# Weight low halves, key rope and convolution blocks rearranged in a two-block transformer kernel

## The chip, the core and the metric

The kernel runs on one core of a Trainium2 chip. The metric is the device time of one execution in microseconds (us); 1730.88 us is the median of three runs before the change, which lay between 1729.36 and 1731.35 us.

## What is computed

The reference is two transformer parts on 256 tokens of width 1024, all in float32:

- a first block: `x + mixed @ w_o`, where `mixed` joins a stick-breaking attention of 8 heads and a latent attention (MLA) of 8 heads, followed by a PEER layer. In MLA each key is `concat(k_nope, k_rot)`: 64 numbers of its own head and 32 numbers, `k_pe`, that all heads share. The key is normalised (`rms_norm` with `k_norm`) and only then the last 32 are turned by `rope`. PEER scores 16 sets of 128 sub-keys with `w_q`, picks 16 experts of 16384 per head by two rounds of `top_k`, and sums `coef * v[idx]`;
- two further layers, each modulated by a vector: layer 0 is a differential attention with a Fourier branch and a SwiGLU, layer 1 a conformer convolution (`a * sigmoid(g)`, a depthwise convolution of 31 taps, layer norm, silu, a projection) and a SwiGLU. A last `rmsnorm` ends it.

## The kernel before, in words

**Split products.** The program works transposed: features on partitions, the 256 tokens along the free axis. Nearly every weight product is made of three rounded products. A weight tile of 128x1024 numbers is loaded, ScalarE copies it to the rounded type (`hi`, `_hi`, L602), and the remainder `src - hi` (`lo`, L615, L644) is the low half. TensorE then adds `hi*x_hi`, `hi*x_lo` and, last, `lo*x_hi` (`steps_t`, L662). So a tile of eight contraction steps is 16 matmuls with `hi`, then 8 with `lo`.

**Who makes the low half.** `plan` (L532) lists every weight tile in the order of use, with a number `cut`: columns below `cut` are made by VectorE, the others by GpSimd (POOL). Before, the cut is 512 (half and half) for the first block's mixer, for six of the 16 `w_pq` tiles and for the differential layer; 0 (all POOL) for the other `w_pq` tiles and the first `EARLY` = 40 of the 128 `peer_u` tiles; 1024 (all VectorE) elsewhere. `next_w` (L628) hands out the next tile and issues loads, `hi` and `lo` ahead: `self.los` says how many tiles ahead the low halves go out.

**Order.** The engines run their queues in order; the order is that in which the Python program issues. In the attention stages `weave` (L237) mixes tasks (one per head) between the steps of a main stream of weight products, by a cost model of TensorE's time.

**First mixer** (`first_mixer`, L835). Query, key and value projections; `kpe` (the shared rope part, L882) is copied by a DMA on the SP queue to all eight heads' keys (L883). `qk_norm` (L1067) is a task per pair of heads, for keys and for queries: square on ScalarE, a product with ones, Ln and Exp on ScalarE, one multiplication on VectorE, then the rope: two VectorE multiplications (32 and 16 rows, 512 columns) and two POOL operations (48 rows). The keys' rope is turned thus four times, once per pair.

**PEER** (`peer`, L1134). 16 `w_pq` tiles; from the fifth on each is followed by the top-16 search of two rows of scores, a chain of short VectorE instructions (`Select.top`, L1925). Then come `EARLY` tiles of `peer_u`, beside which VectorE ends the selection (`selection`, L1181); the rest of `peer_u` runs in pieces of ten matmuls (`mid`, L1214; `steps`, L1238) between the 64 groups that build the coefficient table, three pieces a group, ten pieces before the first (`PRE` = (2, 8)). Last come 128 `peer_v` tiles, beside which the modulation and the context norm (`context`, L1398) are computed.

**Differential layer** (`diff`, L1416). Six query tiles; the rope of a query tile (`rope`, L1435) is four VectorE and two POOL operations, issued two tiles later; then the values (`values`, L1471) and the weave.

**Conformer** (`conformer`, L1728). For each of eight blocks of channels: two weight tiles, a sigmoid gate, and 31 taps that are split over TensorE (diagonal matrices, `conv_pe`, `PE_TAPS`, in plain float32), ScalarE with POOL (`conv_pool`, `POOL_TAPS`) and VectorE (`conv`, the rest). `finish` joins the three; `center`, `square` and `total` make the sums of the layer norm. Then a short serial chain makes its factor, and the projection follows.

Of the kernel before, what the change touches and what calls it, by code (L numbers as in the profile page):

```python
# [16 lines left out]
ALU = mybir.AluOpType  # L17
# [28 lines left out]
PRE = (2,8)  # L46
# [31 lines left out]
def _vec_layout():  # L78
    at = 0
    for name, n in (  # L80
        ("attn_norm", 8), ("cq_norm", 3), ("ckv_norm", 2), ("q_norm", 1), ("k_norm", 1),
# [364 lines left out]
class Net:  # L446
# [85 lines left out]
    def plan(self):  # L532
        a, w = self.a, []
        add = lambda name, cut, *idx: w.append((a[name][idx] if idx else a[name], cut))
        for i in range(6):
            add("w_in", 512, i)
        for i in range(4):
            add("w_sbv", 512, i)
        for kind, i in MAINS:
            if kind == "k":  # L540
                add("w_ukn", 512)
            elif kind == "v":
                add("w_ukv_v", 512)
            elif kind == "m":
                add("w_uq", 512, i)
            else:
                add("w_in", 512, 6 + i)
                add("w_in", 512, 10 + i)
        for name in ("w_om", "w_os"):
            for i in range(4):  # L550
                add(name, 512, i)
        for i in range(16):
            add("w_pq", 512 if i < 6 else 0, i)
# [4 lines left out]
        for i in range(DHEADS):  # L558
            add("ev_qkf", 512, i)
        for i in range(4):  # L560
            add("ev_v", 512, 0, i)
        for i in range(DHEADS):
            add("ev_qkf", 512, DHEADS + i)
        for i in range(4):
            add("ev_v", 512, 1, i)
        for i in range(2):
            add("ev_qkf", 512, 2 * DHEADS + i)
        for i in range(KD):
            add("ev_out", 512, (i + 6) % KD)
# [265 lines left out]
    def first_mixer(self, ctx):  # L835
# [29 lines left out]
        nk = norm(ckv, 2, 15 * U, rk)  # L865
        for i in range(3):
# [16 lines left out]
        nc.sync.dma_start(km[64:QR], self.bc(kpe[64:QR], HEADS))  # L883
# [17 lines left out]
        for _ in rope:  # L901
            pass

# [16 lines left out]
        def main():  # L920
# [72 lines left out]
        for p in range(4):  # L993
            for i, (n, which, x) in enumerate((("k", "k_norm", km), ("q", "q_norm", qm))):
                s = ar(2 * U + (2 * p + i) * 512 if p < 2 else 11 * U + (2 * p + i - 4) * 512, 512)[:QR]
                tasks.append(Task((which, p), self.qk_norm(s, which, x, p, qe if i else ke), [(n, p)], "qk"))
# [70 lines left out]
    def qk_norm(self, sq, which, x, p, ext):  # L1067
# [4 lines left out]
        if "q" in OFFA:  # L1072
            nc.gpsimd.tensor_tensor(sq, xs, xs, op=ALU.mult)
        else:
            nc.scalar.activation(sq, xs, AF.Square)
# [6 lines left out]
        nc.vector.scalar_tensor_tensor(xs, xs, self.vec(which, rows=QR), sq, op0=ALU.mult, op1=ALU.mult)  # L1082
        for o, i in ((slice(64, 96), slice(96, P)), (slice(96, QR), slice(64, 80))):
# [50 lines left out]
    def peer(self, ctx):  # L1134
# [111 lines left out]
        steps(PRE[0])  # L1246
# [853 lines left out]
```

## Time and profile before

| what | value |
|---|---|
| median of three runs | 1730.88 us (1729.36 to 1731.35) |
| the profiled execution's own time | 1729.7 us |
| its span, first to last instruction | 1727.9 us |
| TensorE (PE) busy | 1652.9 us, 96% |
| VectorE (DVE) busy | 1357.9 us, 79% |
| ScalarE (ACT) busy | 1010.0 us, 58% |
| GpSimd (POOL) busy | 418.4 us, 24% |
| mean granted TensorE clock | 0.984 |

The span leaves 1.8 us outside the first and last instruction, and the profiled execution is 1.2 us below the median. Busy shares are means over stages with different limits, so they are read by stage.

### The profile page before, as it was taken

To read this page: it belongs to the slowest core of one execution; us is meant where nothing else is said; L and a number is where in the kernel's file an instruction comes from. 1 tells how busy PE (TensorE), PEld (TensorE's weight loads), DVE (VectorE), ACT (ScalarE), POOL (GpSimd) and SP (SyncE) were. 2 spreads that over 40 slices of the span, in tenths; PEclk is the share of its full clock that TensorE was granted. 3 is DMA by queue.
4 is the path that set the end of the run, shared out by engine and by line. 5 is a ranking of instruction groups with operands and counts; after the bars stand their busy time and mean duration, and the time that the engine had idled before them with its cause. 6 is when DMAs were issued, how large, how long until landed. Compare 5 with 4: busy or idle time off the path is not lost.

```text
span 1727.9 us, 33717 instructions
## 1 busy us (share of the span) xinstructions
PE 1652.9 (96%) x12964; PEld 1580.2 (91%) x12964; DVE 1357.9 (79%) x2395; ACT 1010.0 (58%) x1925; POOL 418.4 (24%) x275
## 2 busy tenths in 40 slices
PE   7989999989999999999999988999999989799998
PEld 6778999989999999999999987788999989699998
DVE  7787899987778875778888778978877799785555
ACT  5756555468777765444555553566555578564444
POOL 3553679910000000000110027533000048410000
PEclk9999999999999999999999999999999999899999
DMA  5332455544445456776878755125788733145553
GB/s 181 117 111 79 135 169 186 175 139 163 159 162 169 160 171 229 248 241 236 299 257 308 271 174 174 52 90 188 273 309 308 261 116 103 50 159 184 185 190 127
DMA packets 88112, 315.66 MB, mean 183 GB/s; under 512 B 10000, under 2 KB 11024, under 8 KB 87696
## 3 DMA queue, kind: packets, MB, share of 16 engines
q1 hardware_dynamic: 87952, 313.51, 53.7%
q8 instruction: 103, 1.69, 0.4%
q14 instruction: 57, 0.47, 0.1%
HBM read 312.03 MB, written 1.05 MB: 181 GB/s over the span
## 4 chain that ended last, share of the span: by engine, by line
PE 63%; DVE 23%; ACT 5%; issue 3%; DMA 3%; POOL 2%; SPq 0%; DVEq 0%; ACTq 0%; POOLq 0%
PE mm L178 34%; PE at L178 28%; DVE a L208 19%; ACT a L208 2%; DMA a<-in_peer_v_dram 2%; ACT wh L208 2%; POOL a L208 1%; DVE praw L208 1%; DMA a<-in_w_dram 1%; DVE xT L208 1%; ACT L208 1%; PE at L183 0%; DVE gb L208 0%; DVE adaw L208 0%; DMA a<-in_w_in_dram 0%
## 5 line engine op out<-in xcount | busy, mean ns | idle before, releaser
L178 PE MATMUL mm<-a,wh 128*128 128x256 f32 (+3 forms) x4752 | 663.7, 289 | 17.0 <-ACT wh L208 11.1
L208 ACT ACTIVATE wh<-a 128x1024 fp32r<-128x1024 f32 (+3 forms) x491 | 514.9, 1053 | 279.1 <-DMA a<-in_w_dram 138.2
L178 PEld LDWEIGHTS mm<-a,wh 128*128 128x128 f32 (+1 forms) x4752 | 608.0, 191 | 33.7 <-ACT wh L208 11.8
L208 DVE TENSOR_TENSOR a<-a,wh 128x1024 fp32r<-128x1024 f32 (+3 forms) x440 | 516.9, 1182 | 118.4 <-ACT wh L208 116.7
L178 PE MATMUL mm<-a,a 128*128 128x256 f32 (+5 forms) x2596 | 415.1, 297 | 24.5 <-DVE a L208 17.7
L178 PEld LDWEIGHTS mm<-a,a 128*128 128x128 f32 (+1 forms) x2596 | 355.2, 191 | 38.5 <-DVE a L208 19.2
L178 PE MATMUL at<-a,wh 128*128 128x256 f32 x2152 | 283.6, 282 | 9.1 <-DVE a L208 5.2
L208 POOL TENSOR_TENSOR a<-a,wh 128x512 fp32r<-128x512 f32 (+3 forms) x118 | 228.0, 1943 | 244.9 <-PE at L178 116.8
L178 PEld LDWEIGHTS at<-a,wh 128*128 128x128 f32 x2152 | 268.4, 190 | 11.7 <-DVE a L208 6.0
L208 POOL TENSOR_TENSOR a<-a 128x256 f32<-128x256 f32 (+3 forms) x44 | 73.6, 1673 | 751.4 <-ACT a L208 749.6
L178 PE MATMUL at<-a,a 128*128 128x256 f32 (+6 forms) x1288 | 211.1, 297 | 5.8 <-POOL a L208 4.3
L178 PEld LDWEIGHTS at<-a,a 128*128 128x128 f32 (+2 forms) x1288 | 171.5, 190 | 22.6 <-issue 9.1
L208 ACT ACTIVATE a<-a 128x256 fp32r<-128x256 f32 (+6 forms) x222 | 100.9, 464 | 110.1 <-DVE a L208 88.1
L208 POOL TENSOR_TENSOR a<-a,a 128x256 f32<-128x256 f32 (+3 forms) x75 | 89.9, 1204 | 304.8 <-ACT a L208 277.5
L208 DVE TENSOR_TENSOR a<-a,a 128x256 fp32r<-128x256 f32 (+5 forms) x191 | 123.7, 648 | 26.0 <-ACT a L208 21.4
L208 ACT ACTIVATE a<-mm 128x256 f32<-128x256 f32 (+30 forms) x170 | 59.0, 351 | 107.3 <-PE mm L178 106.9
L178 PE MATMUL at<-fgh,wh 128*128 128x256 f32 x352 | 86.3, 282 | 2.2 <-ACT wh L208 2.2
L178 PE MATMUL at<-fgl,wh 128*128 128x256 f32 x352 | 86.1, 282 | 0.0
L208 ACT ACTIVATE oh<-oh,rest 128x128 f16<-128x128 f16 x256 | 81.0, 396 | 0.0
L208 DVE TENSOR_TENSOR a<-a,at 128x176 f32<-128x176 f32 (+48 forms) x111 | 36.1, 351 | 54.4 <-PE at L178 34.8
L178 PEld LDWEIGHTS at<-fgh,wh 128*128 128x128 f32 x352 | 66.4, 189 | 2.6 <-ACT wh L208 2.6
L178 PEld LDWEIGHTS at<-fgl,wh 128*128 128x128 f32 x352 | 66.3, 188 | 0.0
(157 smaller groups left out, 1544.9 us busy)
## 6 DMA issues: line engine op xcount, KB each, us to landing
a<-in_w_dram SPq DMA_DIRECT2D x132, 512.0 KB, 4.2
a<-in_peer_u_dram SPq DMA_DIRECT2D x128, 512.0 KB, 3.3
a<-in_peer_v_dram SPq DMA_DIRECT2D x128, 512.0 KB, 4.3
adaw<-in_ada_dram SPq DMA_DIRECT2D x48, 512.0 KB, 4.3
a<-in_ada_dram SPq DMA_DIRECT2D x48, 512.0 KB, 5.1
a<-in_pw_dram SPq DMA_DIRECT2D x24, 512.0 KB, 3.3
a<-in_w_pq_dram SPq DMA_DIRECT2D x16, 512.0 KB, 3.3
a<-in_ev_qkf_dram SPq DMA_DIRECT2D x14, 512.0 KB, 3.4
```

What stands on the lines that cost most here:

```text
L178: return self.engine.matmul(out, w, x, **kw)
L208: return f(*args, **kw)
```

## The change

Seven edits, shortened here where a pattern repeats; `...` marks what is left out.

1. Low halves of all mixer tiles and of all `w_pq` tiles on VectorE; `EARLY` 40 to 44; low halves go out two tiles ahead in the first mixer's projections.
2. The keys' shared part is scaled and turned once, before the attention, and copied to the heads later; `qk_norm` for keys then only scales.
3. The pieces of `mid` ahead of the first group are spread (two after each step).
4. `context` moves one step every four `peer_v` tiles, not every two.
5. The queries' ropes go out beside the values.
6. Ten more convolution taps on TensorE, two fewer on POOL; so VectorE's fall from 97 to 89.
7. The last blocks of the conformer in another order; the layer norm's `r` and `dp` in two PSUM banks; the conformer's `Pre` is set up ahead of the last accumulation.

```diff
-PE_TAPS = (7, 8, 8, 8, 8, 8, 11, 14)
+PE_TAPS = (8, 9, 9, 9, 9, 9, 14, 15)
-POOL_TAPS = (11, 11, 11, 11, 11, 11, 7, 6)
-EARLY = 40
+POOL_TAPS = (11, 11, 11, 11, 11, 9, 7, 6)
+EARLY = 44
-PRE = (2,8)
+PRE = 2
...
         for i in range(6):
-            add("w_in", 512, i)
+            add("w_in", D, i)
...
         for i in range(16):
-            add("w_pq", 512 if i < 6 else 0, i)
+            add("w_pq", D, i)
...
         nk = norm(ckv, 2, 15 * U, rk)
+        self.los = 2
...
-        nc.sync.dma_start(km[64:QR], self.bc(kpe[64:QR], HEADS))
...
         for _ in rope:
             pass
+        self.los = 1
+        kr, kt = ar(0, T), ar(T, T)
+        self.copy(kr[64:QR], kpe[64:QR], scale=self.vec("k_norm")[64:QR])
+        for o, i in ((slice(64, 80), slice(96, QR)), (slice(96, QR), slice(64, 80))):
+            nc.vector.tensor_tensor(kt[o], kr[i], self.sinE[i], op=ALU.mult)
+        nc.vector.tensor_tensor(kr[64:QR], kr[64:QR], self.cosE[64:QR], op=ALU.mult)
+        for o in (slice(64, 80), slice(96, QR)):
+            nc.vector.tensor_tensor(kr[o], kr[o], kt[o], op=ALU.add)
...
                     yield from qk(p)
+                    if p == 0:
+                        nc.sync.dma_start(km[64:QR], self.bc(kr[64:QR], HEADS))
...
-            nc.scalar.activation(sq, xs, AF.Square)
+        n = QR if kpe is None else 64
+        nc.scalar.activation(sq[:n], xs[:n], AF.Square)
+        if kpe is not None:
+            nc.scalar.activation(v3(sq[64:]), self.bc(kpe[64:QR], 2), AF.Square)
...
         nc.vector.scalar_tensor_tensor(xs, xs, self.vec(which, rows=QR), sq, op0=ALU.mult, op1=ALU.mult)
+        if kpe is not None:
+            return
...
-        steps(PRE[0])
+        steps(PRE)
         for g in range(2):
             sel[g].place(slots, g)
+            steps(2)
...
             one_hots(b)
-        steps(PRE[1])
+            steps(2)
...
-            if cg is not None and i % 2 == 1:
+            if cg is not None and i % 4 == 3:
                 next(cg, None)
...
             if i > 1:
-                rope(qT[:, i - 2])
                 next(side, None)
...
         for n, _ in enumerate(values(0, "at")):
-            if n in (1, 3):
-                rope(qT[:, DHEADS - 2 + n // 2])
-            if n % 2 == 0:
+            if n < DHEADS:
+                rope(qT[:, n])
+            else:
                 next(steps, None)
...
+        j = KD - 1
+        self.los = 0
+        pa, ba = pre.scaled(*pre.tile(), sp)
+        conv_pe(j - 1)
+        conv_pool(j - 1)
+        conv(j - 1)
+        square(0, 4)
+        gate(j, pa, ba)
+        total(0, 4)
+        self.copy(ub[j % 2], us[j % 3])
+        finish(j - 2)
+        center(4, 6)
+        conv_pe(j)
+        conv_pool(j)
+        finish(j - 1)
+        conv(j)
+        square(4, 6)
+        total(4, 6)
         self.table(AF.Exp)
...
-        rd = self.bank()
-        r, dp = rd[:, :T], rd[:, T:]
+        r, dp = (self.bank()[:, :T] for _ in range(2))
```

`gate(j, pa, ba)` is the second weight tile of a block with its sigmoid and the gating multiplication, as they stood in the loop. In the loop's last round `center(0, 4)` now goes out ahead of `conv_pool`.

## Rows read from the trace of the kernel before

**Rows 1.** The page's first part: busy time, share of the span, instructions of each engine.
```profile
PE 1652.9 (96%) x12964; PEld 1580.2 (91%) x12964; DVE 1357.9 (79%) x2395; ACT 1010.0 (58%) x1925; POOL 418.4 (24%) x275
```

**Rows 2.** Busy time by stage: stretch, length, PE, PEld, DVE, ACT, POOL (xcount), granted clock.
```profile
52.00:120.00 68.00, 59.97 (x377) 49.79 (x377) 58.32 (x76) 45.21 (x86) 41.44 (x30) 0.92 0.29 91
...
202.70:235.60 32.90, 32.90 (x283) 32.90 (x282) 30.25 (x155) 17.46 (x31) 25.72 (x12) 1.00 0.49 161
235.60:359.40 123.80, 117.59 (x988) 116.61 (x986) 119.33 (x248) 63.08 (x89) 106.67 (x39) 1.00 0.53 175
...
1009.00:1066.00 57.00, 47.43 (x298) 43.92 (x297) 52.09 (x88) 24.78 (x44) 34.14 (x29) 0.94 0.52 176
...
1412.00:1472.00 60.00, 57.58 (x372) 53.24 (x372) 56.23 (x102) 46.26 (x99) 46.28 (x25) 0.97 0.29 95
```

**Rows 3.** The same view for three short stretches with the granted clock at 0.50.
```profile
106.00:112.80 6.80, 6.03 (x25) 5.53 (x25) 6.48 (x16) 4.00 (x7) 2.19 (x3) 0.50 0.22 77
358.60:365.40 6.80, 6.05 (x28) 6.05 (x29) 6.56 (x19) 3.47 (x4) 0.00 (x0) 0.50 0.24 74
1037.80:1044.60 6.80, 5.05 (x23) 5.05 (x24) 5.95 (x12) 2.06 (x5) 4.74 (x5) 0.50 0.32 101
```

**Rows 4.** Timeline at 30 us: start, us, engine, operation [idle before <-releaser].
```profile
29.83 0.68 DVE L208 TENSOR_TENSOR a<-a,wh 128x512 fp32r<-128x512 f32 x1
...
30.57 1.22 PE L178 MATMUL mm<-a,a 128*128 128x256 f32 x4 [0.93 <-DVE a L208]
30.65 1.27 POOL L208 TENSOR_TENSOR a<-a,wh 128x512 fp32r<-128x512 f32 x1 [2.14 <-issue]
...
31.98 1.22 PE L178 MATMUL mm<-a,a 128*128 128x256 f32 x4 [0.18 <-POOL a L208]
```

**Rows 5.** Waits, first mixer, 52 to 120 us: us in total, times, longest.
```profile
PE mm L178 <- DVE a L208: 3.1, 2, 2.4
PE mm L178 <- POOL a L208: 2.7, 3, 1.0
...
PE at L178 <- POOL a L208: 2.2, 1, 2.2
```

**Rows 6.** Groups by form, 52 to 120 us: xcount | busy us, mean ns.
```profile
L208 DVE TENSOR_TENSOR a<-a,a 16x512 f32<-16x512 f32 x8 | 11.4, 1430 | 0.1
L208 DVE TENSOR_TENSOR a<-a,wh 128x512 fp32r<-128x512 f32 x9 | 10.7, 1193 | 3.0 <-ACT wh L208 2.9
L208 DVE TENSOR_TENSOR a<-a,a 32x512 f32<-32x512 f32 x8 | 9.8, 1228 | 0.8
...
L208 POOL TENSOR_TENSOR a<-a,a 48x512 f32<-48x512 f32 x16 | 24.5, 1536 | 3.3 <-DVE a L208 2.2
```

**Rows 7.** Timeline: a whole low half on VectorE with POOL idle.
```profile
1006.06 1.23 DVE L208 TENSOR_TENSOR a<-a,wh 128x1024 fp32r<-128x1024 f32 x1 [1.35 <-ACT wh L208]
```

**Rows 8.** Timeline: TensorE after the early tiles.
```profile
359.35 1.01 PE L178 MATMUL mm<-a,a 128*128 128x256 f32 x3 [4.35 <-DVE a L208]
```

**Rows 9.** Waits, `peer_v` stage, 640 to 1009 us.
```profile
PE at L178 <- ACT wh L208: 3.4, 6, 1.1
```

**Rows 10.** Timeline: the differential layer's fifth query tile.
```profile
1036.94 0.74 PE L178 MATMUL mm<-a,a 128*128 128x258 f32 x4 [2.42 <-DVE a L208]
1039.55 1.23 PE L178 MATMUL mm<-a,a 128*128 128x258 f32 x4 [1.87 <-POOL a L208]
```

**Rows 11.** Waits, query tiles and values, 1009 to 1066 us.
```profile
PE at L178 <- POOL a L208: 2.2, 4, 0.9
```

**Rows 12.** Groups by form, conformer's loop, 1412 to 1472 us.
```profile
L208 DVE SCALAR_TENSOR_TENSOR gb<-at,vecs,gb 128x256 f32<-128x256 f32 x31 | 14.7, 475 | 0.0
```

**Rows 13.** Timeline: TensorE at the conformer's end.
```profile
1472.66 6.31 PE L178 MATMUL mm<-a,a 128*128 128x256 f32 x28 [1.14 <-DVE a L208]
...
1487.11 0.70 PE L178 MATMUL at<-a,cons 128*128 128x256 f32 x2 [3.21 <-POOL a L208]
1488.46 4.05 PE L178 MATMUL at<-a,cons 128*128 128x256 f32 x10 [0.65 <-ACT a L208]
```

More of the change, by code (lines that the diff above doesn't have):

```diff
@@ L993, in first_mixer @@
         for p in range(4):
-            for i, (n, which, x) in enumerate((("k", "k_norm", km), ("q", "q_norm", qm))):
+            for i, (n, which, x) in enumerate((("k", "k_nope", km), ("q", "q_norm", qm))):
                 s = ar(2 * U + (2 * p + i) * 512 if p < 2 else 11 * U + (2 * p + i - 4) * 512, 512)[:QR]
-                tasks.append(Task((which, p), self.qk_norm(s, which, x, p, qe if i else ke), [(n, p)], "qk"))
+                tasks.append(Task((n + "_norm", p), self.qk_norm(s, which, x, p, qe, None if i else kpe), [(n, p)], "qk"))
         for h in range(HEADS):
@@ L1669, in ffn @@
         sp = self.pool("Es", 1, ctx=ctx)
-        diag = self.diag = [ar(3 * U + i * P, P) for i in range(sum(PE_TAPS))] if layer == 0 else None
+        diag = self.diag = [ar((3 * U if i < 72 else 26368 - 72 * P) + i * P, P) for i in range(sum(PE_TAPS))] if layer == 0 else None
         steps = self.steps
@@ L1687, in ffn @@
             if f == NF:
+                if layer == 0:
+                    self.pre = Pre(self, self.xT, *self.modulation(3, 1, 0), 15360, ar(19664, 3, 2, T), ar(21200, T), ar(21504, KD, T), AF.Sigmoid, 5)
                 self.acc_last(acc, cs[-2:])
@@ L1806, in bias, with gate @@
             nc.scalar.activation(self.xT[:, k], self.xT[:, k], AF.Identity, bias=gb[:, k:k + 1])
-        for j in range(KD + 1):
-            if j == KD - 1:
-                self.los = 0
-            if j < KD:
-                pa = pre.tile()
+        def gate(j, pa, ba):
+            pg, bg = pre.scaled(*pre.tile(), sp)
+            if bg is not None:
+                nc.vector.tensor_tensor(bg, bg, self.vec("pw1_b", KD + j), op=ALU.add)
+            g = self.t(sp, [P, T], tag="gsg", bufs=2)
+            self.act(g, pg, AF.Sigmoid, bias=self.vec("pw1_b", KD + j) if bg is None else bg)
+            if j == 0:
+                pre.write()
+            nc.vector.scalar_tensor_tensor(us[j % 3][:, half:half + T], pa, self.vec("pw1_b", j) if ba is None else ba, g, op0=ALU.add, op1=ALU.mult)
+        for j in range(KD - 1):
+            pa = pre.tile()
             if j > 1:
                 conv_pe(j - 1)
-            if j < KD:
-                pa, ba = pre.scaled(*pa, sp)
-                if ba is not None:
-                    nc.vector.tensor_tensor(ba, ba, self.vec("pw1_b", j), op=ALU.add)
-                pg, bg = pre.scaled(*pre.tile(), sp)
-                if bg is not None:
-                    nc.vector.tensor_tensor(bg, bg, self.vec("pw1_b", KD + j), op=ALU.add)
-                s = self.t(sp, [P, T], tag="gsg", bufs=2)
-                self.act(s, pg, AF.Sigmoid, bias=self.vec("pw1_b", KD + j) if bg is None else bg)
-                if j == 0:
-                    pre.write()
-                if j == 6:
-                    self.copy(c, stat[:, :T], scale=1.0 / (3 * P))
-                elif j == 7:
-                    square(0, 3)
-                    square(3, 4)
-                nc.vector.scalar_tensor_tensor(us[j % 3][:, half:half + T], pa, self.vec("pw1_b", j) if ba is None else ba, s, op0=ALU.add, op1=ALU.mult)
+            pa, ba = pre.scaled(*pa, sp)
+            if ba is not None:
+                nc.vector.tensor_tensor(ba, ba, self.vec("pw1_b", j), op=ALU.add)
+            gate(j, pa, ba)
             for _ in range(GW[min(j, 3)]):
```

66 lines of the change are left out of this document (28 added, 38 removed).

## The prediction

> **What bounds the kernel now.** The page's busy table comes first: TensorE is busy for 96% of the span [rows 1]. So a change can win only where TensorE stands still or runs at its lower clock, and must not add to its work. The view of busy time by stage then shows where that is [rows 2]: in the first mixer's middle TensorE is busy for 59.97 of 68 us, at the start of the differential layer for 47.43 of 57, while the weight products of `w_pq` fill all of 32.90 us. The same view for short stretches shows the other loss [rows 3]: from 106.0 and from 1037.8 us the granted clock is 0.50 (1.2 GHz), each time after TensorE had waited more than once.
>
> The waits and the timeline say for whom it waits. A low half made by two engines comes late: VectorE starts its half at 29.83 us and needs 0.68, and only then POOL starts its own, at 30.65, for 1.27 us; TensorE waits for the first and again for the second [rows 4]. Between 52 and 120 us it waits 3.1 us for VectorE, and 2.7 and 2.2 us for POOL [rows 5]; the last is one wait for a rope. At 1036.94 and 1039.55 us it waits 2.42 and 1.87 us for the two halves of one tile [rows 10].
>
> One stage stands against this: beside `w_pq`, VectorE is busy for 30.25 of 32.90 us [rows 2] with 155 short instructions, so its queue is as full as TensorE's, and POOL makes the low halves there.
>
> **The change, part by part**, each against the profiled execution of 1729.7 us.
>
> *Low halves in the first mixer, and the keys' rope.* A whole half on VectorE takes 1.23 us with POOL idle [rows 7], against 0.68 + 0.13 + 1.27 = 2.1 us for the pair [rows 4]: the tile is whole 0.9 us sooner, its first half 0.55 us later. What goes at most: the two POOL terms, 4.9 us; half of the 3.1 us for VectorE, 1.5 [rows 5]; the 0.93 + 0.18 us of rows 4, since a low half two tiles ahead is issued before the rope tables that held it up; and the clock's loss from 106.0 us, half of the 6.03 busy us, 3.0 [rows 3]. That is 10.5 us. VectorE gets 32 tiles x 0.55 = 17.6 us more, and loses four key ropes: half of 11.4 + 9.8 us, 10.6 [rows 6]. POOL loses half of 24.5 us besides its halves [rows 6]. The single turn adds five small VectorE instructions before the attention, some 2 us, covered by the value products; without that cover they would delay the first key pair by as much. ScalarE squares the shared part again in each of four tasks, in a queue with room. The copy of the keys' part is one DMA on SP, moved behind the first query and key tiles; it waits for `kr`, which is long done by then, so the loads behind it are not held; were it late, the first key task would be late next. So the term lies between -10.5 and, with all extra VectorE work on the path, 17.6 - 10.6 = +7. I take -7.5, nearer to the waits, because VectorE's halves now take 1.19 us each beside POOL [rows 6], hardly less than a whole one alone.
>
> The Trainium skill, "SBUF — State Buffer", section "Who interferes with whom", says that a VectorE instruction with two SBUF inputs and a GpSimd one that reads SBUF take turns, and the loser blocks for the whole instruction. By that rule every POOL instruction removed here can give VectorE back its length, and the term would be the whole -10.5. The 1.19 against 0.68 us speak for it; how often the two meet in the new order no row shows.
>
> *The `w_pq` tiles and 44 early tiles.* TensorE passes a tile in 3.29 us (32.90 for ten) [rows 2]. VectorE already needs that time for two rows of search, and now gets 1.23 us more per tile [rows 7], and the next tile's half stands in its queue behind the rows. Ten tiles go in step with VectorE at 4.52 us: +12.3. Four of the six tiles before meet a full queue too, 0.55 each: +2. In return the early stage has four more tiles, 4 x 24 matmuls x 0.119 (117.59 us for 988) = 11.4 us, so VectorE ends its selection in time, and the wait of 4.35 us at 359.35 [rows 8] with the clock's loss behind it, half of 6.05 us [rows 3], goes: -7.4. Net +7 (bounds: 0, if VectorE has room that its 8% idle hides, and +14, if the wait at the end stays).
>
> *Pieces ahead of the first group.* Early tiles up by four leave 83 x 24 = 1992 matmuls in pieces of ten; 12 pieces ahead and 3 per group use them up 1.6 groups before the end, where before 68 were left over, 8 us of cover for the first coefficients. Now one tile's 16 matmuls cover them, 1.9 us, against an estimated 4 us: the low half of 1.23 us [rows 7] behind two multiplications, two copies and two short low halves of some 0.5 us each: +2 (0 to +4).
>
> *Context at half the rate.* Of 3.4 us of waits in that stage [rows 9] about half falls where it runs together with the modulation: -1.5 (0 to -3).
>
> *Differential layer.* Without ropes among the query tiles, the low half of the fifth follows at once: 2.42 + 1.87 us go [rows 10], and the clock's loss from 1037.8 us, half of 5.05 us, 2.5 [rows 3]. The values' POOL waits, 2.2 us [rows 11], go too, but six ropes of four VectorE instructions each now stand there before VectorE's halves; about 1 us of new wait comes. Sum -8; I take -7.5 (-9 to +2). The later key tiles add 0.55 us each to VectorE and free POOL; I cost them at nothing, covered by the main stream's products, which follow each other without a wait on a half there; without that cover five key tiles cost 5 x 0.55 = 2.8 us.
>
> *Conformer's loop.* Both engines are nearly full, 57.58 and 56.23 of 60 us [rows 2]. Six more taps there are 12 matmul records of 0.225 us (6.31 for 28) [rows 13], +2.7; VectorE loses four taps of 0.475 [rows 12], 1.9, which removes some of TensorE's waits for it. Between -1.9 and +2.7, I take +1. The diagonals are made by ScalarE beside the SwiGLU, in slack.
>
> *Conformer's end.* Now TensorE waits 1.14 us for the last gate, then 3.21 and 0.65 us among the sums, which end at 1488.46 + 4.05 = 1492.5 [rows 13]. In the new order the first sums fill the wait for the gate. From 1471.5: three more taps 1.3 us, eight sums 3.6, fifteen taps 6.8, eight last sums 3.6: 1486.8. That is 5.7 us sooner; I take -5 (0 to -7). The two banks may free a few tenths in the serial chain; the earlier set-up too; both at nothing.
>
> Sum: -7.5 + 7 + 2 - 1.5 - 7.5 + 1 - 5 = -11.5, 1718.2 us. The median lay 1.2 us above the profiled execution: **1719.4 us**, 1719.
>
> **The rivals.**
> *VectorE becomes the bound (slower).* Its in-order queue passes TensorE's wherever it takes the low halves: place, the first mixer (58.32 of 68 us now), `w_pq` and the differential layer (52.09 of 57) [rows 2]. Then the mixer costs +7, `w_pq` +14, the differential layer +2: with the other terms 1729.7 + 7 + 14 + 2 + 2 - 1.5 + 1 - 5 = 1749 at worst, 1738 at half that force. It decides from the point where VectorE has no idle time left there. Against it: its instructions are stretched by POOL now, 1.19 against 0.68 us [rows 6].
> *The waits move.* TensorE waits as long for VectorE as for POOL, because the halves queue behind the softmax work; then mixer and differential layer bring only the POOL waits, 4.9 + 1.9 us, and half of that is met by new waits: 1729.7 - 3.4 + 9 - 1.5 + 1 - 5 + 1.2 = 1731. For it: most of the waits in rows 5 and 10 name VectorE at least as often as POOL.
> *The blocked time comes back.* By the rule above: mixer -10.5, differential layer -9, `w_pq` +3: 1711.
>
> **How the numbers follow.** Forecast 0.58, blocked time back 0.16, waits move 0.13, VectorE bound 0.13. What a measurement can tell from no change is 0.2%, 3.5 us. The forecast's own bounds, a few terms wrong at once, are 1712 to 1727; with the two near rivals the range is 1707 to 1733, which leaves out the slow rival and the far ends. Faster by over 0.2% hold the first two cases and a part of the third: 0.75; within 0.2%: 0.11; slower: 0.14.
>
> **What would show it.** Right: no POOL instruction on weight tiles before the early ones; PE waits for POOL near zero before 180 us and between 1009 and 1066; the `w_pq` tiles at about 4.5 us with waits for VectorE between; no wait at the first tile after the early ones; the clock at 1.00 after 1037 us; the conformer's sums ending without a 3 us wait. Wrong: `w_pq` still at 3.3 us a tile; new waits of over 2 us for VectorE in the mixer; conformer's blocks over 10.2 us each.

## The result, and the profile after

The changed kernel takes **1704.91 us** (median of 4 runs, 1702.76 to 1707.44); before, beside it on the same chip, took 1730.12 us. The ratio is 0.9856 (95% interval 0.9838 to 0.9875): faster by 25 us, more than twice the forecast 12, and 2 us below the range. Each set of runs below has its own chip and its own runs of before, so ratios are compared; 0.001 is 1.7 us. A second measurement, made beside later runs, gave 0.9874 (0.9859 to 0.9889) and 1705.32 us:

> The changed kernel itself, as the yardstick of the runs beside it on one chip. Ratio to before 0.984 to 0.9875, the interval of its first measurement.

The mean of the two, 0.9865, is the yardstick below, and a difference under 0.002 from it is not told from none.

**One mistake stands ahead of the prediction, and it is the largest part of the miss.** Edit 1 and the diff there say that the low halves of all 16 `w_pq` tiles go to VectorE. The kernel's line is

```diff
-            add("w_pq", 512 if i < 6 else 0, i)
+            add("w_pq", D if i < 6 else 0, i)
```

so only the first six go there, and the ten later ones stay on POOL. The prediction priced an edit that was not made. (Edit 1 also leaves out that the plan gives the differential layer's low halves to VectorE, which the prediction does price.) Its own test for this ("wrong: `w_pq` still at 3.3 us a tile") is the first thing that the trace answers. The timeline of POOL, and then of TensorE, in the changed kernel:

```profile
202.96 2.40 POOL L208 TENSOR_TENSOR a<-a,wh 128x1024 fp32r<-128x1024 f32 x1 [0.90 <-ACT wh L208]
206.25 2.40 POOL L208 TENSOR_TENSOR a<-a,wh 128x1024 fp32r<-128x1024 f32 x1 [0.90 <-ACT wh L208]
```

```profile
201.26 2.14 PE L178 MATMUL mm<-a,wh 128*128 128x256 f32 x16
...
204.56 2.14 PE L178 MATMUL mm<-a,wh 128*128 128x256 f32 x16
```

Tiles follow each other every 3.30 us (204.56 - 201.26) with no wait, and POOL still makes a whole half for each.

The page's busy line of the changed kernel answers to [rows 1]:

```profile
PE 1642.9 (96%) x12984; PEld 1577.0 (93%) x12984; DVE 1335.9 (78%) x2379; ACT 1012.8 (59%) x1932; POOL 321.9 (19%) x201
```

The profiled execution took 1705.88 us, its span is 1704.1, the mean granted clock 0.991 (before 0.984). The span is 23.8 us shorter. TensorE's idle time fell from 1727.9 - 1652.9 = 75.0 us to 1704.1 - 1642.9 = 61.2, that is by 13.8 us; its busy time fell by 10.0 us although it has 20 records more. So a part of the gain is the **clock**. Half of TensorE's busy time in the stretches at half clock, the estimate that the prediction uses, is 22.1 us before (nine stretches) and 12.2 us after (six): 9.9 us. The prediction had counted three of these stretches, 8.5 us.

How large that part is differs from execution to execution. The second profile of the changed kernel has the same span, 1704.2 us, but eight such stretches and 16.2 us by this estimate, which leaves 5.9 us. The profiled execution of the kernel before was also one with a low clock: 57 other runs of that kernel have a mean clock of 0.987 (0.982 to 0.990) and a mean time of 1727.5 us. So the clock is some quarter to two fifths of the gain, as an estimate.

Busy time by stage, to be held against [rows 2] (first mixer; ten `w_pq` tiles; early tiles; start of the differential layer; conformer's loop):

```profile
52.00:115.00 63.00, 60.68 (x410) 52.66 (x409) 47.65 (x70) 49.80 (x93) 12.46 (x8) 0.97 0.41 124
193.20:226.10 32.90, 32.90 (x282) 32.90 (x282) 30.25 (x154) 17.47 (x32) 24.30 (x11) 1.00 0.50 162
226.10:350.00 123.90, 120.80 (x1012) 119.70 (x1011) 119.59 (x237) 61.61 (x86) 117.06 (x41) 1.00 0.53 177
991.20:1040.00 48.80, 47.01 (x314) 44.59 (x314) 44.62 (x78) 26.61 (x46) 18.52 (x18) 1.00 0.50 173
1393.00:1453.00 60.00, 57.64 (x376) 53.69 (x375) 56.80 (x93) 46.18 (x97) 47.37 (x26) 0.97 0.27 88
```

The first and the fourth lines show the gain: TensorE idle for 2.3 us of 63 where it was 8.0 of 68, and for 1.8 of 48.8 where it was 9.6 of 57, at a higher clock. The second is the same as before to 0.1 us on TensorE and VectorE, as it must be when nothing changed there.

Where the time went, from the starts of the same instructions in both traces (the second profile of the changed kernel in brackets):

| stage, from one mark to the next | forecast | measured |
|---|---|---|
| start to first search (first mixer) | -7.5 | -11.5 (-11.6) |
| first search to first `peer_v` product (selection, pieces) | +9 | -4.9 (-4.8) |
| `peer_v` to first query product (context) | -1.5 | -1.5 (+0.2) |
| query tiles of the differential layer | -7.5 | -8.0 (-8.0) |
| first value product to first feed-forward product | 0 | +2.0 (+3.3) |
| first feed-forward | 0 | +2.9 (+1.3) |
| conformer, to the first product of its projection | -4 | -4.1 (-4.9) |
| rest | 0 | +1.3 (+0.7) |

Rows differ by up to 1.7 us between the two profiles of the same kernel. In the context row the 1.7 us between them is one stretch at half clock, from 833.1 us, which the second profile alone has (half of its 3.40 busy us).

### The profile page after: what moved, and what is told of

Its sections match the earlier page's. It is cut to its first block, busy times and chain, and to the rows that moved or that the text cites. A ratio compares the mean times of both kernels' runs of the same rounds, so it can differ in the third digit from the quotient of the medians.

```text
span 1704.1 us, 33577 instructions
## 1 busy us (share of the span) xinstructions
PE 1642.9 (96%) x12984; PEld 1577.0 (93%) x12984; DVE 1335.9 (78%) x2379; ACT 1012.8 (59%) x1932; POOL 321.9 (19%) x201
## 4 chain that ended last, share of the span: by engine, by line
PE 73%; DVE 11%; ACT 6%; DMA 4%; POOL 3%; issue 2%; SPq 0%; DVEq 0%; ACTq 0%; POOLq 0%
PE mm L178 42%; PE at L178 30%; DVE a L208 9%; ACT a L208 3%; POOL a L208 3%; DMA a<-in_peer_v_dram 2%; ACT wh L208 2%; DMA a<-in_w_dram 1%; DMA a<-in_peer_u_dram 1%; DVE adaw L208 0%; DVE xT L208 0%; ACT L208 0%; DVE gb L208 0%; PE at L183 0%; DMA a<-in_w_in_dram 0%
## 5 line engine op out<-in xcount | busy, mean ns | idle before, releaser
L208 DVE TENSOR_TENSOR a<-a,wh 128x1024 fp32r<-128x1024 f32 (+2 forms) x436 | 539.0, 1243 | 124.2 <-ACT wh L208 123.2
L208 POOL TENSOR_TENSOR a<-a 128x256 f32<-128x256 f32 (+4 forms) x44 | 71.6, 1628 | 852.0 <-ACT a L208 826.6
L208 ACT ACTIVATE a<-a 128x256 fp32r<-128x256 f32 (+8 forms) x225 | 103.1, 469 | 115.4 <-DVE a L208 86.0
L208 POOL TENSOR_TENSOR a<-a,a 128x256 f32<-128x256 f32 (+4 forms) x65 | 77.8, 1201 | 476.6 <-ACT a L208 422.5
L208 POOL TENSOR_TENSOR a<-a,wh 128x1024 fp32r<-128x1024 f32 x54 | 148.6, 2773 | 15.4 <-ACT wh L208 15.2
L208 DVE TENSOR_TENSOR a<-a,a 128x256 fp32r<-128x256 f32 (+6 forms) x188 | 108.3, 577 | 28.7 <-ACT a L208 23.8
L208 DVE TENSOR_TENSOR a<-a,at 128x204 f32<-128x204 f32 (+54 forms) x115 | 36.6, 355 | 48.9 <-PE at L178 42.6
L208 DVE TENSOR_TENSOR fs<-fs,mm 128x256 f32<-128x256 f32 x38 | 16.0, 421 | 74.5 <-PE mm L178 69.0
```

The costliest lines, as they stand in the source:

```text
L208: return f(*args, **kw)
```

## The experiments

**All `w_pq` tiles on VectorE: what the prediction had priced.**

```diff
-            add("w_pq", D if i < 6 else 0, i)
+            add("w_pq", D, i)
```

> The changed kernel (1704.9 us, median), but with the low halves of all 16 w_pq tiles on VectorE. In the changed kernel the trace shows that only the first six are there: POOL still makes the other ten, and TensorE passes a tile in 3.29 us. The prediction had priced all sixteen on VectorE at +12.3 us for these ten tiles. Theory A (the price was right and only the plan was misread): the ten tiles go at some 4.5 us, TensorE waits for VectorE between them, the first search starts to drift, and the run is 1713 to 1718 us (+8 to +13, less what VectorE makes good under the early tiles). Theory B (VectorE had room and the price was wrong too): the tiles stay at 3.3 us and the run is 1704 to 1707 us.

Ratio 0.9945 (0.9930 to 0.9959), 1718.25 us: 14 us slower than the changed kernel. Theory A, at the upper edge of its range. Timeline of TensorE in this run:

```profile
207.49 1.21 PE L178 MATMUL mm<-a,a 128*128 128x256 f32 x8 [0.99 <-DVE a L208]
...
212.04 1.21 PE L178 MATMUL mm<-a,a 128*128 128x256 f32 x8 [1.00 <-DVE a L208]
```

A tile now takes 4.55 us (212.04 - 207.49; the forecast was 4.52), with a wait for VectorE in each. From the first search to the first `peer_v` product this run takes 453.5 us, the changed kernel 439.4: 14 us, where +12.3 was priced. So the price was right; the kernel that was changed was another. This run is the kernel that the prediction describes. That its gain in all, 9.5 us, is near the forecast 11.5 is partly luck: in its trace the mixer brings 11.3 us and not 7.5, and 4.9 us that the prediction has at nothing are lost behind the first value product, outside the conformer.

**The first mixer, its two edits apart.** In the changed kernel, its low halves (not `w_pq`) back to half and half:

```diff
-            add("w_in", D, i)
+            add("w_in", 512, i)
...
```

> The changed kernel with the low halves of the first mixer (input, value, key, query and output tiles) half on VectorE and half on POOL again; the first six w_pq tiles stay on VectorE, and the keys' shared part is still turned once. Theory A (the waits for the late second half were the mixer's loss): most of the 11.5 us that the first mixer won is given back, 1711 to 1716 us, and TensorE waits for POOL and VectorE again between 60 and 110 us. Theory B (the keys' rope, which held both engines, was the loss): at most 3 us are given back, 1704 to 1708 us.

and, separately, the keys' rope turned per pair again:

```diff
+        nc.sync.dma_start(km[64:QR], self.bc(kpe[64:QR], HEADS))
...
-                tasks.append(Task((n + "_norm", p), self.qk_norm(s, which, x, p, qe, None if i else kpe), [(n, p)], "qk"))
+                tasks.append(Task((n + "_norm", p), self.qk_norm(s, which, x, p, qe if i else ke), [(n, p)], "qk"))
```

> The changed kernel with the keys' rope turned four times again, once per pair of heads, and the shared part copied to the heads at its old place; the mixer's low halves stay on VectorE. Theory A (low halves alone bring the mixer's gain): 1704 to 1708 us. Theory B (VectorE can take the low halves only because it lost the key ropes): 10 us more of work on VectorE lie on TensorE's path in part, 1710 to 1716 us, with waits for VectorE between 60 and 120 us.

Ratios 0.9938 (0.9919 to 0.9958) and 0.9920 (0.9906 to 0.9934): 13 and 9.5 us slower. Theory A of the first and theory B of the second hold, so each loses most of what both had won. Since that seemed to say that neither pays alone, both were put on the kernel before, one tile ahead, and the low halves there by themselves:

```diff
-            add("w_in", 512, i)
+            add("w_in", D, i)
...
+        kr, kt = ar(0, T), ar(T, T)
...
```

> The kernel before with two edits only: the first mixer's low halves on VectorE, one tile ahead, and the keys' shared part turned once. In the changed kernel the first search starts 11.5 us earlier, and 15.7 us earlier with one tile ahead. Theory A (that gain is the mixer's own and stays to the end): 12 to 16 us faster than before, ratio 0.991 to 0.993. Theory B (with 40 early tiles and the old half split behind it, VectorE's selection gives part of it back): 0.994 to 0.997, with a longer wait than 4.35 us at the end of the early tiles.

> The kernel before with one edit only: the first mixer's low halves on VectorE; the keys' rope is still turned per pair. Theory A (the two edits pay only together, as undoing either one in the changed kernel says): within 3 us of before, ratio 0.998 to 1.002. Theory B (the low halves alone take away the waits for POOL): 5 to 8 us faster, 0.9955 to 0.997.

Both together: 0.9931 (0.9919 to 0.9944), 12 us faster than before; the first search starts 15.2 us earlier, and the end of the trace is 15.4 us earlier, so the gain is kept (theory A). The low halves alone: 0.9970 (0.9959 to 0.9981), 5 us by the runs, 8.6 us at the first search. That is theory B: the low halves do pay alone, and the rope adds 6.6 us (15.2 - 8.6). In both runs the trace shows 3 us more than the runs do: the one trace of before is from an execution 2 us above the mean of the others. That the two pay only together is therefore wrong; the run with halves and a single turn, whose first search is 2.8 us later than before, also had its halves two tiles ahead. The run with the rope per pair starts its first search at 198.9 us, that of the low halves alone at 191.9; ahead of it the two differ by the lead and the first six `w_pq` tiles, so the lead probably hid most of the gain there, though no run shows that by itself.

Why VectorE had room for more work shows in the groups by form and the stage's busy time. First the run with the rope per pair (52 to 120 us), which differs from [rows 6] in the mixer by the low halves and their lead alone:

```profile
L208 DVE TENSOR_TENSOR a<-a,wh 128x1024 fp32r<-128x1024 f32 x10 | 13.0, 1297 | 2.7 <-ACT wh L208 2.7
L208 DVE TENSOR_TENSOR a<-a,a 32x512 f32<-32x512 f32 x8 | 7.3, 912 | 0.8
L208 DVE TENSOR_TENSOR a<-a,a 16x512 f32<-16x512 f32 x8 | 5.5, 684 | 0.1
```

```profile
52.00:120.00 68.00, 58.99 (x386) 50.00 (x385) 58.34 (x79) 45.98 (x88) 24.73 (x16) 0.95 0.29 92
```

Ten whole halves cost 13.0 us where nine half ones cost 10.7, and the same rope multiplications fell from 1430 and 1228 ns to 684 and 912, 8.5 us in all. VectorE is as busy as before, 58.34 against 58.32 us, with the low halves on it. The Trainium skill, "SBUF — State Buffer", section "Who interferes with whom", says that a VectorE instruction with two SBUF inputs and a GpSimd one that reads SBUF exclude each other for a whole instruction; these rows agree with it, as VectorE's instructions are shorter where POOL has fewer. So do the instructions one by one. Of the eight multiplications of 16 rows before, the two with no POOL instruction beside them took 0.68 us, the six others 1.66 to 1.69; in the run with the rope per pair none of the eight met one, and all took 0.68 to 0.69. The timeline shows a pair of rope multiplications (32 rows, then 16) before, with POOL at work,

```profile
92.89 3.29 POOL L208 TENSOR_TENSOR a<-a,a 48x512 f32<-48x512 f32 x2
93.47 3.26 DVE L208 TENSOR_TENSOR a<-a,a 32x512 f32<-32x512 f32 x2
```

and one in the run with the rope per pair, with POOL idle:

```profile
91.30 1.39 DVE L208 TENSOR_TENSOR a<-a,a 32x512 f32<-32x512 f32 x2
```

The single turn then takes half the rope multiplications and POOL's share of them away. In the changed kernel (52 to 115 us):

```profile
L208 DVE TENSOR_TENSOR a<-a,a 32x512 f32<-32x512 f32 x4 | 3.7, 926 | 0.2
...
L208 DVE TENSOR_TENSOR a<-a,a 16x512 f32<-16x512 f32 x4 | 2.7, 685 | 0.1
```

VectorE is at 47.65 of 63 us there, the first room it has had in this stage. The waits of TensorE at the run with the rope per pair (60 to 150 us) show what that room was worth:

```profile
PE mm L178 <- DVE a L208: 5.6, 2, 3.9
PE at L178 <- DVE se L208: 4.4, 4, 1.5
PE at L178 <- POOL a L208: 2.0, 1, 2.0
```

The 3.9 us is a wait for a low half that stood behind softmax work: the rival "the waits move", which was right for half of the edit.

**Low halves one tile ahead in the first projections.**

```diff
-        self.los = 2
+        self.los = 1
```

> The changed kernel with the first mixer's low halves issued one tile ahead and not two during its first projections. Theory A (two ahead removes waits at 30 us, as the prediction said): 1 to 3 us are lost, 1706 to 1708 us. Theory B (a low half issued early waits for ScalarE's rounded copy at the head of VectorE's queue, and the scaling of the key latents behind it comes late: TensorE waits 2.22 and 2.47 us at 33.2 and 36.4 us): those waits shrink to under 1.5 us together, the clock's stretch at half from 35.0 us goes or moves, 1699 to 1703 us.

Ratio 0.9840 (0.9824 to 0.9857), 4 us faster than the yardstick: theory B. The timeline of TensorE in the changed kernel, and then in this run:

```profile
28.77 1.13 PE L178 MATMUL mm<-a,cons 128*128 128x256 f32 x4 [1.31 <-POOL a L208]
...
33.17 0.73 PE L178 MATMUL mm<-a,wh 128*112 128x256 f32 x4 [2.22 <-DVE a L208]
36.38 0.98 PE L178 MATMUL mm<-a,wh 128*112 128x256 f32 x3 [2.47 <-DVE a L208]
```

```profile
28.66 2.01 PE L178 MATMUL mm<-a,a 128*128 128x256 f32 x8 [2.81 <-DVE a L208]
...
31.81 2.40 PE L178 MATMUL mm<-a,wh 128*112 128x256 f32 x16
```

With the lead of two, VectorE's queue has two low halves of 1.22 us, at 30.44 and at 34.43, ahead of the scaled input that TensorE needs first, and it stood idle for 1.31 us before the second, for ScalarE's rounded copy; 33.17 and 36.38 are the two results. VectorE's row of the second in the changed kernel:

```profile
34.43 1.22 DVE L208 TENSOR_TENSOR a<-a,wh 128x1024 fp32r<-128x1024 f32 x1 [1.31 <-ACT wh L208]
```

With a lead of one there is one wait of 2.81 us in this stretch, and the first search comes 4.2 us earlier. The prediction had counted the lead as a gain.

**The early tiles.** 40 in the changed kernel, then 40 in a later version (`e14_one_ahead_pre_late`, below):

```diff
-EARLY = 44
+EARLY = 40
```

> The changed kernel with 40 early tiles of peer_u, as before, and not 44. Theory A (four more tiles let VectorE end its selection in time): TensorE waits 3 to 5 us at the first tile after the early ones and its granted clock falls to 0.50 for the 6 to 7 us behind it; the run is 1709 to 1713 us (+4 to +8 against 1704.9). Theory B (the two pieces after each step now cover that end, wherever it lies): no wait over 1 us there and 1703 to 1706 us.

> The version with one tile ahead and the late set-up (ratio 0.9843 in its runs), with 40 early tiles and not 44. Theory A (the four tiles are worth what the trace of the changed kernel with 40 shows up to the peer_v stage, 3.4 us): ratio 0.9860 to 0.9875, a wait of 2 to 4 us at the first tile after the early ones. Theory B (they only move where TensorE waits, as the whole span of that run said, 1.5 us shorter): 0.9835 to 0.9850.

Ratios 0.9889 (0.9875 to 0.9902) and, against 0.9843 with 44, 0.9866 (0.9850 to 0.9883): 4 us both times, though each interval overlaps one of those that it is held against. Timeline of TensorE in the second run:

```profile
343.13 0.74 PE L178 MATMUL mm<-a,a 128*128 128x256 f32 x4 [4.17 <-DVE a L208]
```

The wait of [rows 8] is back. In the first run it is 2.71 us, less than expected, and that profiled execution is 1.5 us shorter as a whole than the one with 44, against its runs; up to the first `peer_v` product it is 3.4 us longer. From the first search to the first `peer_v` product the four tiles bring 3.1 us in the first pair of traces and 3.8 in the second. With 44 tiles the longest wait left there is one of 1.28 us for POOL. Theory A, with 4 us in place of the 7.4 us forecast.

**The first six `w_pq` tiles**, half and half again.

```diff
-            add("w_pq", D if i < 6 else 0, i)
+            add("w_pq", 512 if i < 6 else 0, i)
```

> The changed kernel with the low halves of the first six w_pq tiles half on VectorE and half on POOL, as before; the other ten stay on POOL. Theory A (the first six are in the way of VectorE's queue, as the prediction priced four of them, +2 us): the run is 1702 to 1704 us. Theory B (the pair comes later than the whole and six tiles gain as the mixer does): 1706 to 1709 us, with waits for POOL at the first tiles. No difference (1704 to 1706 us) says that the ScalarE copy ahead of these tiles is last there.

Ratio 0.9881 (0.9862 to 0.9900), 3 us slower in the mean, which is not told from none. In the trace the first search starts at 191.2 us, and at 188.9 to 190.2 in nine traces with the same mixer and whole halves, so some 1 to 2 us later; there is no wait for POOL, and one of 0.35 us for VectorE, at 191.28 us. Theory B in sign at most; its mechanism was not seen.

**The differential layer.** Ropes among the query tiles, and low halves half and half, each in the changed kernel:

```diff
             if i > 1:
+                rope(qT[:, i - 2])
                 next(side, None)
...
```

> The changed kernel with the queries' ropes back among the query tiles of the differential layer; its low halves stay on VectorE. Theory A (the ropes on VectorE held up the low half of the fifth query tile): TensorE waits 2 to 4 us for VectorE between 1005 and 1030 us, the granted clock falls behind it, and the run is 1709 to 1713 us (1704.9 us for the changed kernel). Theory B (it was the half on POOL that came late): no wait over 1 us and 1704 to 1707 us.

> The changed kernel with the differential layer's low halves half on VectorE and half on POOL again; the ropes stay beside the values. Theory A (the ropes' place alone brings the layer's gain): 1704 to 1707 us. Theory B (the halves bring it): TensorE waits for POOL at the query tiles or the values, 1709 to 1713 us. From the first mixer, where either half of the edit alone gave back nearly everything, a third outcome is likely: both matter, and this run and the one with the ropes among the queries give back 8 us each.

0.9909 (0.9894 to 0.9925), 8 us slower: the ropes' place is the gain (the run also has the old places of the other steps beside the values). 0.9863 (0.9843 to 0.9884): the low halves make no difference in the whole. Both theories A; the third outcome did not come. With the ropes among the queries, TensorE's timeline reads

```profile
1020.58 1.25 PE L178 MATMUL mm<-a,a 128*128 128x258 f32 x8 [2.96 <-DVE a L208]
...
1025.62 2.08 PE L178 MATMUL mm<-a,a 128*128 128x256 f32 x8 [1.89 <-DVE a L208]
```

and the changed kernel's waits between 991 and 1040 us are only

```profile
PE mm L178 <- ACT wh L208: 0.9, 1, 0.9
PE mm L178 <- DVE a L208: 0.8, 2, 0.6
```

against [rows 10, 11]. The zero for the low halves is two effects of opposite sign. With halves, the query tiles take 3.9 us more (26.5 against 22.6; the 2.6 in a text further down is too low) and the stretch from the first value product to the first feed-forward product 5.0 us less. In the changed kernel the woven order ends with the last head's norm alone, as its timeline of TensorE shows:

```profile
1152.31 1.99 PE L178 MATMUL at<-daT,a 128*128 128x256 f32 x8 [0.22 <-ACT daT L208]
1155.43 1.12 PE L178 MATMUL at<-a,cons 128*128 128x512 f32 x2 [1.13 <-ACT a L208]
1159.45 1.47 PE L178 MATMUL mm<-a,wh 128*128 128x256 f32 x4 [2.89 <-ACT a L208]
```

In the run with halves the same two products with `cons` stand ahead of output tiles, and no wait follows:

```profile
1158.75 1.02 PE L178 MATMUL at<-a,cons 128*128 128x512 f32 x2
1159.21 1.04 PE L178 MATMUL mm<-a,wh 128*128 128x256 f32 x4
```

**The conformer.** The old split of the taps; and the old order of the blocks with the new split.

```diff
-PE_TAPS = (8, 9, 9, 9, 9, 9, 14, 15)
+PE_TAPS = (7, 8, 8, 8, 8, 8, 11, 14)
...
```

> The changed kernel with the convolution's taps split between the engines as before (ten fewer on TensorE, two more on POOL); the new order of the conformer's end stays. Theory A (the taps as the prediction priced them): TensorE has 20 matmul records fewer, 4.5 us, of which some two thirds come back as waits for VectorE in the loop; the run is within 3 us of the changed kernel, 1702 to 1708 us. Theory B (the taps unload VectorE at the conformer's end, and the new order needs that): VectorE ends its last taps later and TensorE waits for it ahead of the last sums, 1708 to 1713 us.

> The changed kernel with the conformer's blocks in the order of before, all nine rounds in one loop with the first sums behind the last taps; the new split of the taps and the two banks stay. Theory A (the order brings the end's gain): TensorE waits again 3 us for the squares' operands among the sums, and the run is 1708 to 1712 us (+3 to +7 against 1704.9). Theory B (the taps bring it): 1703 to 1706 us.

Ratios 0.9871 (0.9851 to 0.9891) and 0.9886 (0.9866 to 0.9905). The taps make no difference that can be told (theory A); the order is worth 3 to 4 us (theory A's low end; its interval overlaps the second measurement of the yardstick, so the trace has to carry it): the conformer, from its first product to the projection's, takes 104.9 us in the changed kernel, 108.3 with the old order, 104.5 with the old taps and 109.0 before. TensorE at the conformer's end in the changed kernel, and then with the old order:

```profile
1453.29 3.61 PE L178 MATMUL at<-a,cons 128*128 128x256 f32 x16
1456.74 6.67 PE L178 MATMUL mm<-a,a 128*128 128x256 f32 x30
1463.25 2.75 PE L178 MATMUL at<-a,cons 128*128 128x256 f32 x12
1466.26 1.15 PE L178 MATMUL at<-a,cons 128*128 128x256 f32 x4 [0.26 <-DVE a L208]
1472.04 3.79 PE L178 MATMUL at<-a,wh 128*128 128x256 f32 x16 [4.64 <-DVE a L208]
```

```profile
1453.61 6.75 PE L178 MATMUL mm<-a,a 128*128 128x256 f32 x30 [1.14 <-DVE a L208]
...
1466.12 0.70 PE L178 MATMUL at<-a,cons 128*128 128x256 f32 x2 [1.45 <-POOL a L208]
1467.47 2.43 PE L178 MATMUL at<-a,cons 128*128 128x256 f32 x10 [0.65 <-ACT a L208]
```

The first sums fill the wait for the last gate, and the waits among the sums of [rows 13] are gone. The serial chain behind them, 4.64 us of wait ahead of the projection, is the same in both and in the kernel before, so the two banks brought nothing there.

**The conformer's set-up behind the last accumulation.**

```diff
-                if layer == 0:
-                    self.pre = Pre(...)
                 self.acc_last(acc, cs[-2:])
...
         if layer == 0:
+            self.pre = Pre(...)
```

> The changed kernel with the set-up of the conformer's normalised input behind the last accumulation of the first feed-forward again, as before. In the changed kernel TensorE waits 2.69 us for VectorE there, just ahead of that accumulation, and its clock is 0.50 for 3.4 us behind it; before it had no wait of over 0.2 us there. Theory A (the set-up, now ahead in VectorE's queue, holds up the last low half): that wait and the clock's loss go, and nothing takes their place: 1700 to 1703 us. Theory B (the set-up then comes late for the conformer's first tile, which was hidden by the early start): the wait moves to the conformer's first matmul, 1704 to 1707 us.

Ratio 0.9874 (0.9854 to 0.9895): not told from the yardstick. In the trace the wait of the changed kernel becomes a smaller one and one of 0.81 us at the conformer's first product, with the clock at full: its first product comes 3.7 us sooner after the first `fgh` product. The rows are TensorE in the changed kernel, VectorE in it, and TensorE in this run:

```profile
1362.47 0.55 PE L178 MATMUL at<-fgh,a 128*128 128x256 f32 x2 [2.69 <-DVE a L208]
```

```profile
1361.10 0.18 DVE L208 TENSOR_TENSOR a<-mods,a 128x16 fp32r<-128x16 f32 x1 [1.64 <-ACT a L208]
1361.19 2.35 DVE L208 TENSOR_TENSOR a<-a,wh 128x1024 fp32r<-128x1024 f32 x2
```

```profile
1360.74 0.50 PE L178 MATMUL at<-fgh,a 128*128 128x256 f32 x2 [0.58 <-DVE a L208]
```

The set-up's instruction waits 1.64 us for ScalarE at the head of VectorE's queue, and the last low halves stand behind it. By the trace theory A in part; by the runs alone it stays open.

**A version that beats both.** One tile ahead and the late set-up (the two diffs above); then, in it, the differential layer's low halves on VectorE only up to the first values, and half and half throughout.

```diff
-            add("ev_qkf", D, DHEADS + i)
+            add("ev_qkf", 512, DHEADS + i)
...
-            add("ev_out", D, (i + 6) % KD)
+            add("ev_out", 512, (i + 6) % KD)
```

> The version that the runs so far point to: the changed kernel with the first projections' low halves one tile ahead (4 us sooner at the first search in its trace) and the conformer's set-up behind the last accumulation (some 3 us sooner at the conformer's first matmul in its trace, though its runs took as long). If both add: 1697 to 1700 us by the ratio to before, 0.981 to 0.983. If only the first counts: 1700 to 1703 us.

> The version with one tile ahead and the late set-up (ratio 0.9843), with the differential layer's low halves on VectorE only for the six query tiles and the first half of the values; the later tiles are half and half again. In the run with the whole layer half and half TensorE lost 2.6 us at the query tiles but won 5 us between the values and the feed-forward, where the last head's norm then lies ahead of the last output tiles and not behind them. Theory A (both can be had): first feed-forward tile 4 to 6 us after that of the version compared, taken from the first value tile on, and a ratio of 0.9815 to 0.983. Theory B (the order at the layer's end hangs on the order at its start): the waits of 1.1 and 2.9 us at the layer's end stay and the ratio is 0.984 to 0.9855.

> The same version with all of the differential layer's low halves half and half. Theory A (as in the changed kernel, where it made no difference): ratio 0.9835 to 0.985. Theory B (it is better by the 2 to 3 us by which the layer's end gains more than its start loses): 0.9815 to 0.983.

(In the second text "4 to 6 us after that" is a slip for "4 to 6 us sooner than that".) Ratios 0.9843 (0.9826 to 0.9860), **0.9816** (0.9795 to 0.9836; 1696.26 us beside 1726.76 before) and 0.9830 (0.9811 to 0.9850). In the first, only one edit counts in the runs. In the second both effects of the differential layer are had: from the first value product to the first feed-forward product it takes 144.6 us against 148.4 in the first, 3.8 us less (theory A had 4 to 6), and the waits of 1.13 and 2.89 us are gone. Its ratio lies in theory A's range, and its interval lies below both intervals of the changed kernel. The third lies between, and its interval does not tell theory A from theory B.

## Why the prediction was right and wrong

**Low halves and rope in the first mixer (-7.5; -11.5 measured).** The mechanism was right, the size not. The step that failed is the clock's loss, "from 106.0 us, half of the 6.03 busy us, 3.0". The kernel before had three more stretches at half clock in this stage, which were not counted (busy time of stretches, as in [rows 3]):

```profile
82.10:85.50 3.40, 3.40 (x12) 2.06 (x10) 3.36 (x3) 1.12 (x2) 2.92 (x2) 0.50 0.17 13
177.70:184.50 6.80, 6.35 (x29) 6.24 (x30) 5.50 (x10) 5.17 (x9) 2.13 (x2) 0.50 0.24 77
27.50:34.30 6.80, 5.68 (x23) 4.83 (x22) 6.70 (x12) 2.08 (x3) 3.30 (x4) 0.50 0.31 49
```

The changed kernel has two:

```profile
35.00:41.80 6.80, 5.42 (x18) 4.83 (x19) 5.53 (x17) 3.02 (x6) 0.18 (x1) 0.50 0.21 64
103.30:106.70 3.40, 3.40 (x18) 3.31 (x16) 3.35 (x5) 2.94 (x10) 0.85 (x1) 0.50 0.00 0
```

Half of the busy time is (3.40 + 6.35 + 5.68 + 6.03) / 2 = 10.7 us before and (5.42 + 3.40) / 2 = 4.4 after: 6.3 us for the clock. TensorE's waits from 24 us to the first search, all rows of the view of waits added, fell from 16.9 us to 13.0, 3.9 us. Together that is 10.2 of the 11.5. (Before has one trace, and its clock was low, so its share for the clock may be too high.) Two errors partly met: the lead of two tiles cost 4 us where it was counted as a gain of 0.93 + 0.18, and low halves with the single turn, one tile ahead, bring 12 us by the runs and 15.2 in the trace, above the 10.5 that the prediction called the most. The bound of +7, extra VectorE work on the path, was the wrong fear, since VectorE's other instructions shrank by nearly as much as it was given (58.34 us busy against 58.32 in the run with the rope per pair).

**`w_pq` and 44 early tiles (+7), pieces (+2): -4.9 measured.** The failed step is "ten tiles go in step with VectorE at 4.52 us: +12.3": no such tile exists in the changed kernel. With that step left out and nothing else altered, this part is -7.4 + 2 + 2 = -3.4, the whole sum -7.5 - 3.4 - 1.5 - 7.5 + 1 - 5 = -23.9, and the time 1729.7 - 23.9 + 1.2 = 1707.0 us, where 1704.9 was measured. That this is so near is partly luck: the mixer and this part came out 5.5 us better than their terms, and the three rows that were at nothing 6.2 us worse. The 44 tiles brought 4 us, not 7.4. The first six tiles whole, priced at +2 for four of them, cost nothing that shows; the trace has them 1 to 2 us to the good, and the runs do not tell it from none. The pieces were not tried by themselves; with 40 tiles the stage took 1 to 2 us less than before, so no run shows their +2.

**Context (-1.5).** -1.5 in one profile, +0.2 in the other; not tried by itself. In the 17 traces with the new rate this stage takes 366.6 to 370.4 us, in the three with the old one (before, and the two runs made on it) 368.4 to 370.6, so no effect of it is told.

**Differential layer (-7.5).** -8.0 at the query tiles, through the ropes' place, as argued: no wait at the fifth tile, and no stretch at half clock there. The key tiles "at nothing" failed: the low halves changed the woven order, and 5 us at the layer's end were lost with them.

**Conformer (+1 and -5).** -4.1 in sum. The order gave 3 to 4 us, as argued: the 3.21 us wait among the sums is gone. The taps gave nothing that can be told. "The earlier set-up too; both at nothing" failed: the set-up stood ahead of the last low halves, where before it stood behind them, and TensorE waited 2.69 us.

**The rivals.** As the prediction put them, "VectorE becomes the bound" is what happens if all `w_pq` tiles go to VectorE, 14 us, but not in the mixer. "The waits move" holds for the low halves without the single turn, and its support was misread: [rows 5] shows two waits for VectorE and four for POOL. "The blocked time comes back", 1711 us, had the mechanism of the mixer; its sum carried the same misread tiles.

## What to carry to other kernels

Price the line that was changed, with its condition: one `if` was worth 14 us here. When a wait goes, look for every stretch at half clock behind it, not for the largest alone; some quarter to two fifths of this gain was clock. But take the clock's share from several traces, since two of the same kernel differed by 4 us in it. And an instruction that is issued early and must itself wait holds up all that stands behind it in its queue: the low half two tiles ahead and the early set-up both did, for 4 and 3 us in the traces.

## What the runs showed of the hardware that was not expected

Moving work from POOL to VectorE left VectorE no busier: nine half tiles and sixteen rope multiplications took 31.9 us beside POOL's low halves (10.7 + 11.4 + 9.8), ten whole tiles and the same multiplications 25.8 us without them (13.0 + 7.3 + 5.5).

And the same waits do not always bring the lower clock. Ahead of the first search TensorE waited 1.17 and 0.71 us before, and the clock fell to 0.50 for 6.8 us. The changed kernel waits 0.93 and 1.08 us at the same products, and the clock stayed at full. But ten traces have that mixer, two tiles ahead, each with waits of 0.93 to 0.94 and 1.08 to 1.09 us there: in three of them the clock fell to 0.50 for 3.4 us at the second wait, in seven it did not. The changed kernel, and then the run with the old order of the conformer, with its granted clock behind the wait:

```profile
170.00 0.79 PE L178 MATMUL mm<-a,wh 128*128 128x256 f32 x2 [1.08 <-ACT a L208]
```

```profile
169.49 0.90 PE L178 MATMUL mm<-a,wh 128*128 128x256 f32 x2 [1.09 <-ACT a L208]
```

```profile
170.00:173.40 3.40, 3.40 (x17) 3.40 (x18) 3.22 (x6) 3.22 (x7) 0.00 (x0) 0.50 0.00 0
```

So the stretches at half clock of one trace are one draw, and a change is not to be judged by whether one of them went in a single pair of traces.
